# A two-layer hybrid encoder: second feed-forward product in seven block products, S5 tables a layer ahead, convolution in 32-wide tiles

## The chip, the cores and the metric

One NeuronCore of a Trainium2 chip runs the whole program. TensorE (PE) multiplies; its weight loads are listed apart as PEld. VectorE (DVE), ScalarE (ACT) and GpSimd (POOL) do elementwise work, SyncE (SP) issues all DMAs here. The metric is device time in microseconds (us), the median of several runs. A profile comes from one further execution.

## The reference

Two layers (`DEPTH = 2`), 1024 tokens, width 1024. A layer projects x to four head groups, joins them, and ends in a gated feed-forward part:

```python
h = jnp.einsum('bsd,de->bse', x, w_in[l])
y_a = conformer_conv(h[..., :OFF_S5], ...)      # GLU, depthwise conv of 31 taps, LayerNorm, silu
y_b = s5_mixer(h[..., OFF_S5:OFF_SC], ...)      # 16 groups, 64 complex states, both directions
y_c = short_gated_conv(h[..., OFF_SC:OFF_DA], sc_conv_w[l])
y_d = diff_attention(q, k, v, lam, da_subln_g[l], lam_init)   # 4 heads, two softmax maps each
mix = jnp.einsum('bse,ed->bsd', jnp.concatenate([y_a, y_b, y_c, y_d], axis=-1), w_out[l])
x = layer_norm(DEEPNORM_ALPHA * x + mix, ln1_g[l], ln1_b[l])
ff = jax.nn.silu(x @ w_ffn1[l]) * (x @ w_ffn3[l])
x = layer_norm(DEEPNORM_ALPHA * x + ff @ w_ffn2[l], ln2_g[l], ln2_b[l])
```

All is float32; the hidden width `FFN` is 2816, that is 22 blocks of 128.

## The kernel before

**Precision.** A large product is made of three: each operand is split into a rounded high part and the low rest (`split`, a cast and a subtraction), and `mm3` (L546) issues high by high, high by low and low by high, each a matmul of 128 rows, 128 columns of weights and up to 512 moving columns. Small products run in plain float32, where one matmul shows as two records.

**Order.** Every call goes through `Weaver`, which records it and then orders all instructions of the program by its own estimates, with a shift of priority for each step and layer (`SHIFT`) and a preference for the engine of an operation that several can do (`PREF`; `any2` is VectorE or GpSimd, `any3` also ScalarE). The result is a fixed list for each engine, worked off in that order. All instructions carry the line of `emit` (L471), so they are told apart by tile names.

**Stages of a layer.** `mixers_in` (L1519) runs through nine blocks of `w_in`: `tg` are token-major products, `cg` channel-major ones. Between them stand the S5 pairs: `s5_pair_tables` (L868) computes tables of a pair of groups (tile `s5t`), `s5_pair` (L926) uses them. The convolution (`conv_windows`, `conv_part`, `conv_norm`, L1068 to L1104) is a matmul for each of 256 channels (`cvo`): weights are a Toeplitz block of 128 rows and 96 columns, read by DMA with overlapping rows, and 11 windows of tokens move. Then come attention (`sc` scores, `atp` transposes, `po`) and the output product (`wo`), interleaved row block by row block.

**Feed-forward part.** `run` (L1581) goes over 11 chunks of 256 hidden columns. For w_ffn1 (q = 0) and w_ffn3 (q = 1), `ffn_up` (L1458) makes each 2 by 2 block product out of seven block products (`up`) instead of eight; `make_unit` (L1424) forms the seven weight operands of a group with four additions and splits each into one of four slots of `wring`. A group's raw weights (`upraw`) come in two buffers, which are reloaded once read. The second product (`dn`, `ffn_down` L1496) is direct: it is woven between the groups, chunk by chunk, each time adding to the rows in SBUF (`r`):

```python
for ci, (g, w2) in enumerate(chunks):
    for i in range(2):
        self.mm3(ps, g[:, 0, i, ts], g[:, 1, i, ts], w2[i][:, 0, :], w2[i][:, 1, :],
                 ci == 0 and i == 0, ci == len(chunks) - 1 and i == 1)
```

The last two chunks are added together, row block by row block, each followed by its LayerNorm.

Of the kernel before, what the change touches and what calls it, by code (L numbers as in the profile page):

```python
# [9 lines left out]
F32 = mybir.dt.float32  # L10
# [35 lines left out]
R_SW, R_LG, R_LB, R_GB, NROW = 0, 3, 4, 5, 6  # L46


CB, CWIN, NBLK, CG = 96, 128, 11, 9
NCK = -(-GW // CG)  # L50
WROW = CB + CWIN
CBANK = 43
# [16 lines left out]
class Weaver:  # L69
# [3 lines left out]
    SHIFT = {"None": -3232, "attn_finish0": 525, "attn_finish1": -8000, "attn_heads0": 2951, "attn_heads1": -4395,  # L73
# [12 lines left out]
    PREF = {"attn_finish0 gpsimd": -4310, "attn_finish0 scalar": -769, "attn_finish0 vector": 4528,  # L86
# [20 lines left out]
    CHUNK = 1370.0  # L107
    WINDOW = 3413.0
    SHARE = 0.42
    OUTS = ("out",)  # L110

# [373 lines left out]
class Trunk:  # L485
# [164 lines left out]
    def load_small(self, l):  # L650
# [3 lines left out]
        for r, k in ((R_LG, "conf_ln_g"), (R_LB, "conf_ln_b"), (R_GB, "s5_b_glu")):  # L654
            nc.sync.dma_start(raw[r:r + 1, :], t[k][l:l + 1, :])
# [735 lines left out]
    def weight_stream(self, l, order):  # L1391
# [3 lines left out]
        for item in order:  # L1395
# [4 lines left out]
            for u in range(n):  # L1400
                makers.append((g, u, u == n - 1))
# [318 lines left out]
```

## Time and profile before

| what | value |
|---|---|
| median of 3 runs | 2551.14 us (2549.97 to 2555.72) |
| the profiled execution, own time | 2548.31 us |
| its span, first to last instruction | 2546.5 us |
| TensorE busy | 2438.0 us, 96% |
| VectorE, GpSimd, ScalarE busy | 63%, 49%, 31% |
| mean granted TensorE clock | 0.964 of full |
| DMA | 193.53 MB, mean 76 GB/s |

A busy TensorE is not TensorE at its peak: its busy time is stretched where the granted clock is lower. A matmul's duration overlaps that of the next, so what one costs is read from the distance between starts, or from a group's busy time by its count.

### The profile page before, as it was taken

Reading aid. Unit: us, or ns where it says so; the run is one execution under the profiler, and the core shown is the slowest. Engines: PE = TensorE matmul, PEld = TensorE weight load, DVE = VectorE, ACT = ScalarE, POOL = GpSimd, SP = SyncE. Lnnn points to the kernel's source line nnn. Section 1 sums busy time; section 2 is a strip of 40 time slices with the busy share of each in tenths; the row PEclk is TensorE's granted clock in tenths of the full one; section 3 lists DMA queues with packets and bytes.
Section 4 is the critical chain, followed back from the end, with each engine's and each line's share of the span. In section 5 each row is a group of like instructions: output and inputs, shape, how many; then the busy total and the mean of one; then the engine's idle time right before and its main releaser. Section 6 shows DMA issues by size and latency. Waiting matters only on the chain. (4 is left out here: it accounts for less than half of the span.)

```text
span 2546.5 us, 34450 instructions
## 1 busy us (share of the span) xinstructions
PE 2438.0 (96%) x13464; PEld 2049.7 (80%) x13464; DVE 1592.5 (63%) x2559; ACT 795.2 (31%) x1343; POOL 1243.4 (49%) x1015
## 2 busy tenths in 40 slices
PE   8999989888999999999899999899989999999997
PEld 7889987677888888888688899777778888888885
DVE  6688348886555555555563785698855445554456
ACT  2200356543222222222231113555432222222231
POOL 2201373535566666565640004745376655555574
PEclk9998899999999999999899989999999999999998
DMA  6334321114111111111333342211241111111212
GB/s 165 100 90 132 98 73 51 60 51 155 53 53 55 50 50 58 51 53 55 113 114 85 85 124 91 73 63 55 72 132 58 53 56 52 56 50 50 58 53 96
DMA packets 193081, 193.53 MB, mean 76 GB/s; under 512 B 84878, under 2 KB 168088, under 8 KB 192664
## 3 DMA queue, kind: packets, MB, share of 16 engines
q1 hardware_dynamic: 192920, 191.34, 24.9%
q8 instruction: 106, 1.74, 0.3%
q14 instruction: 55, 0.45, 0.1%
HBM read 164.61 MB, written 26.71 MB: 75 GB/s over the span
## 5 line engine op out<-in xcount | busy, mean ns | idle before, releaser
L471 PE MATMUL up<-xT,wring 128*128 128x512 f32 x2112 | 485.9, 389 | 0.0
L471 PEld LDWEIGHTS up<-xT,wring 128*128 128x128 f32 x2112 | 396.4, 188 | 82.3
L471 PE MATMUL dn<-wring,g 128*128 128x512 f32 x1920 | 450.4, 391 | 3.9 <-POOL wring L471 3.1
L471 POOL TENSOR_TENSOR wring<-upraw,wring 128x512 fp32r<-128x512 f32 x220 | 311.5, 1418 | 250.4 <-ACT wring L471 250.1
L471 PEld LDWEIGHTS dn<-wring,g 128*128 128x128 f32 x1920 | 359.8, 188 | 83.3 <-POOL wring L471 6.6
L471 PE MATMUL up<-xB,wring 128*128 128x512 f32 x1584 | 370.0, 389 | 0.2 <-DVE xT L471 0.2
L471 PEld LDWEIGHTS up<-xB,wring 128*128 128x128 f32 x1584 | 297.3, 188 | 62.1 <-DVE xT L471 0.4
L471 DVE TENSOR_TENSOR r<-r,dn 128x512 f32<-128x512 f32 x288 | 197.9, 687 | 214.0 <-PE dn L471 214.0
L471 ACT CAST wring<-upraw 128x512 fp32r<-128x512 f32 x220 | 136.6, 621 | 469.8 <-PE dn L471 162.5
L471 PE MATMUL cg<-xh,win 128*128 128x512 f32 x640 | 220.9, 414 | 3.1 <-POOL win L471 1.9
L471 PE MATMUL tg<-win,xh 128*128 128x256 f32 x1024 | 203.0, 296 | 1.0 <-POOL win L471 0.6
L471 PE MATMUL wo<-wout,yhl 128*128 128x512 f32 x768 | 195.8, 400 | 0.0
L471 PEld LDWEIGHTS tg<-win,xh 128*128 128x128 f32 x1024 | 170.5, 202 | 3.2 <-POOL win L471 0.9
L471 ACT ACTIVATE probs<-sc,asm 128x1024 f32<-128x1024 f32 x128 | 143.2, 1120 | 91.8 <-DVE asm L471 91.7
L471 DVE TENSOR_REDUCE asm<-sc 128x1 f32<-128x1024 f32 x128 | 155.3, 1217 | 24.7 <-PE sc L471 24.3
L471 PEld LDWEIGHTS wo<-wout,yhl 128*128 128x128 f32 x768 | 142.1, 190 | 28.8 <-POOL yhl L471 0.3
L471 POOL TENSOR_TENSOR wring<-w2raw,wring 128x512 fp32r<-128x512 f32 x80 | 103.7, 1301 | 105.0 <-ACT wring L471 105.0
L471 PE MATMUL tg<-win,xl 128*128 128x256 f32 x512 | 153.2, 300 | 0.0
L471 PEld LDWEIGHTS cg<-xh,win 128*128 128x128 f32 x640 | 126.0, 197 | 32.7 <-issue 2.9
L471 POOL CAST win<-wraw 128x1024 fp32r<-128x1024 f32 x21 | 27.8, 1326 | 212.6 <-PE cg L471 160.1
L471 PE MATMUL cg<-xl,win 128*128 128x512 f32 x320 | 129.5, 405 | 0.0
L471 POOL TENSOR_TENSOR wring<-tw,wring 128x512 fp32r<-128x512 f32 x88 | 122.7, 1394 | 7.8 <-ACT wring L471 7.8
(232 smaller groups left out, 3851.1 us busy)
## 6 DMA issues: line engine op xcount, KB each, us to landing
upraw<-in_w_ffn_dram SPq DMA_DIRECT2D x88, 512.0 KB, 3.8
w2raw<-in_w_ffn_dram SPq DMA_DIRECT2D x44, 512.0 KB, 3.5
wraw<-in_w_in_dram SPq DMA_DIRECT2D x36, 512.0 KB, 4.5
ctap<-taps_scr SPq DMA_DIRECT2D x38, 432.0 KB, 4.9
woraw<-in_w_out_dram SPq DMA_DIRECT2D x16, 512.0 KB, 3.7
r<-x_scr SPq DMA_DIRECT2D x16, 512.0 KB, 4.0
conv<-taps_scr SPq DMA_DIRECT2D x18, 432.0 KB, 4.8
x_scr<-xr SPq DMA_DIRECT2D x14, 512.0 KB, 3.0
```

What stands on the lines that cost most here:

```text
L471: getattr(e, method)(*args, **kwargs)
```

## The change

**Second product in two phases.** `ffn_up` now runs over all 11 chunks first. Its products (`gst`) and four sums or differences of them (`down_operands`) are stored to memory (`a_scr`). Then the down phase takes seven block products, one after the other, each over 11 chunks: a unit n is 4 row tiles by one chunk, 12 matmuls. `down_prep`, called three units ahead, loads the unit's left operand (`araw`), forms the weight difference where there is one, and splits both sides into `aring` and `wring`; `down_out` adds a finished block product to the rows it belongs to. Rows are normalised after the sixth and the seventh product, four row blocks each.

**S5 tables.** Those of the second layer are computed during the first layer's chunks 0 to 7 and stored; the second layer loads them.

**Convolution.** A channel is now a matmul of 64 rows and 32 columns with 32 windows moving; two row halves and four column groups of the array alternate. The transposes that make the windows (`cvw`) go from 44 to 136. The normalisation over channels sums with a small matmul. **Order of blocks:** attention's v, q, k instead of k, v, q. The tables `SHIFT` and `PREF` have other numbers throughout.

```diff
-CB, CWIN, NBLK, CG = 96, 128, 11, 9
...
+CB, CWIN, NBLK, WROW = 32, 64, 32, 96
...
-    SHIFT = {"None": -3232, "attn_finish0": 525, "attn_finish1": -8000, "attn_heads0": 2951, "attn_heads1": -4395,
...
+    SHIFT = {"None": -7481, "attn_finish0": 1069, "attn_finish1": -7446, "attn_heads0": 1472, "attn_heads1": -6174,
...
+    def s5_ahead(self, l, pr):
...
+        self.s5_pair_tables(pr, False)
+        self.s5_store(pr)
...
+    def s5_store(self, pr):
+        self.nc.sync.dma_start(self.t5d[pr], self.s5t[pr % 2]["all"])
+
+    @step
+    def s5_load(self, pr):
+        R = self.s5t[pr % 2]
+        self.nc.sync.dma_start(R["all"], self.t5d[pr])
+        self.nc.sync.dma_start(R["M0"], self.m0d[pr].rearrange("j p g n -> (j p) g n"))
...
-                nc.tensor.matmul(ps[0:CB, h, (c - c0) * NBLK:(c - c0 + 1) * NBLK], lhsT=tap[:, k * CB:k * CB + CB], rhs=self.zT[:, :, c], start=True, stop=True)
...
+        for w0 in range(-2, NBLK, 4):
+            ps = self.b((P, 4, P), "cvw")
+            for i in range(min(4, NBLK - w0)):
...
+    def conv_part(self, l, ct):
...
+        for kb in (0, 32):
+            for a in range(2):
+                src = self.wrd[2 * l + ct, 64 * a + kb:64 * a + kb + 1, :]
+                nc.sync.dma_start(self.tapt[64 * a:64 * a + 64], bass.AP(src.tensor, src.offset, [[1, CWIN], [WROW, 32], [1, CB]]))
+            for k in range(kb, kb + 32):
+                j = k % 4
+                for a in range(2):
+                    r = slice(64 * a, 64 * a + 64)
+                    nc.tensor.matmul(ps[32 * j:32 * j + 32, a, k // 4, :], lhsT=self.zT[r, 64 * ct + k, :], rhs=self.tapt[r, k - kb, :],
+                                     start=True, stop=True)
...
-                nc.any2.tensor_tensor(s, s, dst, op=ALU.mult)
-                hi, lo = (rg[:, f, h].rearrange("p (i t s) -> p t i s", t=2, s=P)[:, t] for f in range(2))
-                self.split(s.rearrange("p (i s) -> p i s", s=P), hi, lo)
+                hv = lambda x: x.rearrange("p (r n) -> p r n", r=2)
+                nc.any2.tensor_tensor(G[:, h, :, t], hv(s), hv(dst), op=ALU.mult)
...
-    def ffn_down(self, chunks, j, n, r, first):
...
+    def down_operands(self, c, G, ad):
...
+        op = lambda o, a, b, f: nc.any2.tensor_tensor(U[:, o], U[:, a], U[:, b], op=f)
+        nc.sync.dma_start(ad[c, 0], U[:, 0])
+        op(4, 1, 3, ALU.add)
+        op(6, 0, 1, ALU.subtract)
+        op(5, 4, 0, ALU.subtract)
+        op(7, 2, 5, ALU.subtract)
...
+    DOWN = (("B11", 0), ("B21", 2), ("T1", 4), ("T3", 6), ("T2", 5), ("T4", 3), ("B22", 7))
...
+        b, u = self.DOWN[m]
+        if n % 2 == 0:
+            self.araw = self.raw([P, 2, 512], "araw")
+        a = self.araw[:, n % 2]
+        nc.sync.dma_start(a, ad[c, u])
+        w = lambda k: self.w2u(k, c)
+        if b in ("T1", "T3", "T2", "T4"):
+            x, y = {"T1": ("B12", "B11"), "T3": ("B22", "B12"), "T2": ("B22", "T1"), "T4": ("T2", "B21")}[b]
+            nc.any2.tensor_tensor(w(y), w(x), w(y), op=ALU.subtract)
+        sa, sb = self.aring[:, n % 4], self.bring[:, n % 4]
+        self.split(a, sa[:, 0], sa[:, 1])
+        self.split(w(b), sb[:, 0], sb[:, 1])
...
+        sa, sb = self.aring[:, n % 4], self.bring[:, n % 4]
+        for i in range(4):
+            s = slice(i * P, i * P + P)
+            self.mm3(ps[i], sa[:, 0, s], sa[:, 1, s], sb[:, 0], sb[:, 1], c == 0, c == NHID // 2 - 1)
...
+            elif m == 4:
+                add(r(0, i, 1), p)
+                add(u[i], p)
+                axpy(r(1, i, 0), u[i])
+                nc.any2.tensor_tensor(r(1, i, 1), r(1, i, 1), u[i], op=ALU.add)
...
-        return [OFF_S5, 0, GW, OFF_SC + GW, OFF_SC + 2 * GW, OFF_SC, OFF_DA + GW, OFF_DA + 2 * GW, OFF_DA]
+        return [OFF_S5, 0, GW, OFF_SC + GW, OFF_SC + 2 * GW, OFF_SC, OFF_DA + 2 * GW, OFF_DA, OFF_DA + GW]
...
-        self.s5_pair_tables(0)
+        tables = self.s5_pair_tables if l == 0 else self.s5_load
...
-            if pr % 3 == 0:
-                self.conv_part(l, pr // 3)
+            if pr < 2:
+                self.conv_part(l, pr)
+            elif pr == 3:
+                self.conv_norm(l, yT)
...
-        self.conv_norm(l, yT)
         for jp in range(4):
-            self.attn_k(xT, w(6), jp)
+            self.attn_v(xT, w(6), jp)
...
-            order = [("up", 0, 0), ("up", 0, 1)]
-            for c in range(1, NC):
-                order += [("up", c, 0)] + ([("down", c - 1)] if c < NC - 1 else []) + [("up", c, 1)]
-            self.weight_stream(l, order + [("down", NC - 2)])
...
+            self.weight_stream(l, [(c, q) for c in range(NC) for q in range(2)])
...
+            if l + 1 < DEPTH:
+                self.s5_ahead_alloc(l + 1)
             for c in range(NC):
...
+                self.ffn_up(1, X, sg, G)
+                self.down_operands(c, G, ad)
+                if l + 1 < DEPTH and c < 8:
+                    self.s5_ahead(l + 1, c)
...
+                if n + 3 < 7 * NC:
+                    self.down_prep(n + 3, ad)
...
+                self.down_unit(n, ps)
...
+                    if m >= 5:
+                        for i in range(4):
+                            j = 4 * (m == 5) + tile_of[i]
+                            self.layer_norm(rj(j), g2, b2, out[j] if l + 1 == DEPTH else x2d[j], 1 + (m == 6))
```

How the order moves. TensorE, the first layer's feed-forward part, chunks 0 and 1; first before (`up` and `dn` as above), then with the change (`s5wp` and `s5k` belong to the tables of the second layer):

```order
L471 MATMUL up_650<-xT_480_561,wring_597 128x512 x12
L471 MATMUL up_651<-xT_482_563,wring_597 128x512 x12
L471 MATMUL dn_655<-wring_597,g_598 128x512 x6
L471 MATMUL dn_656<-wring_597,g_598 128x512 x6
L471 MATMUL dn_657<-wring_597,g_598 128x512 x6
```

```order
L473 MATMUL up_656<-xB_492_577,wring_612 128x512 x6
L473 MATMUL s5wp_657<-ident,s5a_636 128x128 x4
L473 MATMUL up_656<-xB_492_577,wring_612 128x512 x6
L473 MATMUL s5k_658<-s5a_635,s5a_636 48x144 x4
L473 MATMUL up_661<-xB_487_572,wring_612 128x512 x12
```

Groups of `up` now follow each other without `dn` between them, with eight small matmuls for the tables once a chunk.

SyncE's queue in the same place; before (`w2raw` are raw weights of the second product), then with the change:

```order
L471 DMA upraw_636<-in_w_ffn_dram 128x4x256
L471 DMA upraw_637<-in_w_ffn_dram 128x4x256
L471 DMA w2raw_647<-in_w_ffn_dram 128x1024
L471 DMA w2raw_648<-in_w_ffn_dram 128x1024
L471 DMA upraw_653<-in_w_ffn_dram 128x4x256
```

```order
L473 DMA s5t_scr<-s5a_635 128x1600
L473 DMA m_scr<-s5a_636 16x8x128
L473 DMA upraw_664<-in_w_ffn_dram 128x4x256
L473 DMA m_scr<-s5a_636 16x8x128
L473 DMA a_scr<-gst_634 128x512
L473 DMA upraw_665<-in_w_ffn_dram 128x4x256
L473 DMA a_scr<-gst_634 128x6x512
L473 DMA upraw_673<-in_w_ffn_dram 128x4x256
```

The loads of raw weights now stand behind stores of tables and of products.

TensorE where attention of the first layer begins; before, then with the change (`ktp` and `qtp` transpose k and q):

```order
L471 MATMUL tg_272<-win_88,xl_7_87 128x256
L471 MATMUL tg_272<-win_88,xh_5_85 128x256 x2
L471 MATMUL sc_297<-kst_154_235,stg_234 128x512 x2
L471 MATMUL sc_298<-kst_154_235,stg_234 128x512 x2
L471 MATMUL tg_272<-win_88,xl_7_87 128x256
```

```order
L473 MATMUL tg_285<-win_92,xl_7_91 128x256
L473 MATMUL ktp_281<-ident,stg_264 128x128 x4
...
L473 MATMUL ktp_290<-ident,stg_264 128x128 x4
L473 MATMUL qtp_308<-ident,stg_264 128x128 x4
L473 MATMUL qtp_309<-ident,stg_264 128x128 x4
L473 MATMUL sc_312<-kst_180_265,stg_264 128x512 x2
```

Before, 85 matmuls of `tg` stand behind the first `sc`, between the scores of the first row block; with the change all `tg` stand ahead of it.

## Rows read from the trace of the kernel before

**Rows 1.** The profile's first part: busy time, share of the span, instructions.
```profile
span 2546.5 us, 34450 instructions
PE 2438.0 (96%) x13464; PEld 2049.7 (80%) x13464; DVE 1592.5 (63%) x2559; ACT 795.2 (31%) x1343; POOL 1243.4 (49%) x1015
```
**Rows 2.** Windows: length, busy time (instructions) per engine, granted clock, DMA share, GB/s.
```profile
core 0: us, PE busy (x) PEld busy (x) DVE busy (x) ACT busy (x) POOL busy (x), PEclk, DMA share, GB/s
110.00:300.00 190.00, 189.31 (x1319) 171.17 (x1318) 133.46 (x303) 26.78 (x54) 34.23 (x42) 0.87 0.39 104
260.00:270.00 10.00, 10.00 (x57) 10.00 (x57) 3.75 (x10) 0.00 (x0) 0.00 (x0) 0.50 0.77 201
350.00:400.00 50.00, 39.08 (x297) 32.66 (x296) 41.06 (x46) 31.43 (x57) 33.82 (x34) 0.93 0.22 72
1360.00:1540.00 180.00, 179.90 (x1242) 160.70 (x1241) 127.63 (x300) 28.60 (x52) 2.96 (x8) 0.88 0.39 105
1866.80:2480.00 613.20, 613.20 (x2707) 507.71 (x2706) 306.51 (x384) 180.19 (x301) 378.95 (x276) 1.00 0.18 55
```
**Rows 3.** The chain of waits, in the second feed-forward part: start, length, what.
```profile
1866.84 54.46 PE up L471 x240
1921.30 10.88 PE dn L471 x48
```
**Rows 4.** Groups by form on PE: tiles, shapes, count | busy us, mean ns.
```profile
L471 PE MATMUL dn<-wring,g 128*128 128x512 f32 x1920 | 450.4, 391 | 3.9 <-POOL wring L471 3.1 <-DVE r L471 0.8
L471 PE MATMUL dn<-w2b,g 128*128 128x512 f32 x192 | 55.6, 425 | 8.8 <-DVE w2b L471 5.5 <-POOL w2b L471 3.2
L471 PE MATMUL cvo<-convz,ctap 128*96 128x11 f32 x700 | 72.7, 245 | 0.0
L471 PE MATMUL cvo<-convz,conv 128*96 128x11 f32 x324 | 35.2, 248 | 0.0
L471 PE MATMUL po<-aT,vq 128*64 128x128 f32 x1024 | 64.9, 280 | 0.0
L471 PE MATMUL cvw<-ident,conv 128*128 128x128 f32 x44 | 6.2, 273 | 0.1
```
**Rows 5.** Timeline of PE: start, length, instruction; three places.
```profile
36.95 1.13 PE L471 MATMUL s5cps<-ident,s5b 16*128 16x16 f32 x16
...
347.22 0.40 PE L471 MATMUL tg<-win,xh 128*128 128x256 f32 x2
347.46 0.28 PE L471 MATMUL tg<-win,xl 128*128 128x256 f32 x1
347.58 0.40 PE L471 MATMUL tg<-win,xh 128*128 128x256 f32 x2
```
**Rows 6.** Windows of the convolution's matmuls alone (tile cvo): PE, PEld, DVE busy, clock.
```profile
170.00:190.00 20.00, 6.98 (x80) 7.11 (x80) 0.00 (x0) 1.00 0.46 122
```
**Rows 7.** Timeline of POOL, second layer's feed-forward part.
```profile
1897.37 1.29 POOL L471 TENSOR_TENSOR wring<-upraw,wring 128x512 fp32r<-128x512 f32 x1 [0.80 <-ACT wring L471]
1900.56 1.29 POOL L471 TENSOR_TENSOR tw<-upraw,upraw 128x512 f32<-128x512 f32 x1 [1.90 <-DMA upraw<-in_w_ffn_dram]
...
1908.64 1.74 POOL L471 TENSOR_TENSOR wring<-upraw,wring 128x512 fp32r<-128x512 f32 x1
```
**Rows 8.** Groups by form on DVE.
```profile
L471 DVE TENSOR_TENSOR xc<-x1row 128x512 f32<-128x512 f32 x4 | 2.7, 674 | 0.0
L471 DVE TENSOR_TENSOR sg<-sg,tw 128x512 f32<-128x512 f32 x66 | 101.5, 1537 | 1.6
L471 DVE TENSOR_TENSOR tu<-tu,up 128x512 f32<-128x512 f32 x110 | 75.0, 682 | 24.7 <-PE up L471 23.6
L471 DVE TENSOR_TENSOR s5t<-P 128x256 f32<-128x256 f32 x94 | 42.0, 461 | 1.4
```
**Rows 9.** Timeline, ends of the two feed-forward parts.
```profile
1231.70 1.20 PE L471 MATMUL dn<-wring,g 128*128 128x512 f32 x4
...
1249.54 1.54 PE L471 MATMUL dn<-w2b,g 128*128 128x512 f32 x6
```
**Rows 10.** Timeline, the last matmuls and the last rows' normalisation.
```profile
2532.15 1.52 PE L471 MATMUL dn<-w2b,g 128*128 128x512 f32 x6
...
2541.50 1.41 DVE L471 SCALAR_TENSOR_TENSOR r<-r,rs,ln 128x512 f32<-128x512 f32 x2 [0.46 <-POOL rs L471]
```

More of the change, by code (lines that the diff above doesn't have):

```diff
@@ L264, in cost @@
                 return max(85.0, 0.4167 * n + 13.3), 0
-            pair = int(outs[0].shape[0]) == 64
-            return max(128.0, 0.4167 * 4 * n + 5) * (0.57 if pair else 1.0), 0
+            k, m = int(kw["lhsT"].shape[0]), int(outs[0].shape[0])
+            if k == 64 and m == 32:
+                return 40.0, 0
+            return max(128.0, 0.4167 * 4 * n + 5) * (0.57 if m == 64 else 1.0), 0
         if eng == "sync":
@@ L867, in s5_pair_tables @@
     @step
-    def s5_pair_tables(self, pr):
+    def s5_pair_tables(self, pr, here=True):
         nc = self.nc
@@ L1017, in conv_alloc @@
         T = self.convt = self.S([P, SROW], F32, "conv")
[L1019 removed]
+        self.zp = [T[:, c * 1040:c * 1040 + 1040] for c in range(2)]
         for z in self.zp:
             self.nc.gpsimd.memset(z[:, 0:16], 0.0)
[L1022 removed]
     def z_half(self, ct, hf):
@@ new lines, in conv_part @@
+    @step
+    def conv_part(self, l, ct):
+        nc = self.nc
+        ps = self.d((P, 2, 16, CB), "cvo")
+        for kb in (0, 32):
[8 more added lines that the diff above has]
+                                     start=True, stop=True)
+        y = self.zTt[:, 1024 * ct:1024 * ct + 1024].rearrange("p (a s t) -> p a s t", a=2, t=CB)
+        cb = self.cb[:, 32 * ct:32 * ct + 32].rearrange("p (a s) -> p a s", a=2)
+        for a in range(2):
+            nc.vector.tensor_tensor(y[:, a], ps[:, a], cb[:, a].unsqueeze(2).to_broadcast([P, 16, CB]), op=ALU.add)
@@ L1133, in conv_norm @@
-        for ct in range(2):
-            nc.sync.dma_start(yT[ct].rearrange("p (j c) -> p j c", j=NJ), out[ct])
+        nc = self.nc
+        v = nc.vector
+        yT_ = lambda t: t.rearrange("p (s t) -> p t s", t=CB)
+        y, q, o = self.zTt[:, 0:2048], self.zTt[:, 2048:SROW], self.zTt[:, 2048:SROW]
+        st = self.cst
+        gsum = lambda ps, x: nc.tensor.matmul(ps, lhsT=self.grp4.rearrange("p j w -> p (j w)"), rhs=x, start=True, stop=True)
+        bc = lambda x: x.unsqueeze(1).to_broadcast([P, 64, CB])
@@ new lines, in conv_norm @@
+        nc.gpsimd.tensor_tensor(st[:, 3], st[:, 3], self.cexp, op=ALU.pow)
+        xn = q.rearrange("p (t s) -> p t s", t=CB)
+        v.tensor_tensor(xn.rearrange("p t s -> p s t"), yv, bc(st[:, 3]), op=ALU.mult)
+        o = y.rearrange("p (j e c) -> p j e c", j=4, e=4)
+        for th in range(4):
+            ps = self.b((P, 4, 4, CB), "cvb")
+            for e in range(4):
+                t0 = 8 * th + 2 * e
+                self.tr(ps[:, e].rearrange("p j w -> p (j w)"), xn[:, t0:t0 + 2, :].rearrange("p t s -> p (t s)"))
+            for j in range(4):
+                nc.scalar.activation(o[:, j, :, 3 - th::4], ps[:, :, j, :], AF.Silu, scale=self.cprm[:, 0, j:j + 1], bias=self.cprm[:, 1, j:j + 1])
@@ L1137, in short_c @@
+        for h in range(2):
+            dst = yT[0:2].rearrange("q p (a n) -> (q p) a n", a=NJ)[:, 7 - h::-2, :]
+            nc.sync.dma_start(dst.rearrange("(s j) e n -> s j e n", j=4), o[64 * h:64 * h + 64])
     @step
@@ L1398, in weight_stream @@
                 prev["next"] = g
-            n = 7 if item[0] == "up" else 4
-            for u in range(n):
-                makers.append((g, u, u == n - 1))
+            for u in range(7):
+                makers.append((g, u, u == 6))
             prev = g
@@ L1549, in mixers_in @@
         self.s5_ring()
-        self.s5_pair_tables(0)
+        tables = self.s5_pair_tables if l == 0 else self.s5_load
+        tables(0)
         nxt(2)
@@ L1558, in mixers_in @@
         gi = 0
-        self.conv_windows(l)
+        for ct in range(2):
+            self.conv_windows(l, ct)
         for pr in range(8):
-            if pr % 3 == 0:
-                self.conv_part(l, pr // 3)
+            if pr < 2:
+                self.conv_part(l, pr)
+            elif pr == 3:
+                self.conv_norm(l, yT)
             self.s5_pair(pr)
             if pr + 2 < 8:
-                self.s5_pair_tables(pr + 2)
+                tables(pr + 2)
             e = len(gem) * (pr + 1) // 8
@@ L1624, in run @@
             self.wring = self.S([P, 4, 2, 512], F32R, "wring")
-            rg = self.S([P, 2, 2, SEQ], F32R, "g")
-            r = [self.S([P, 4, D], F32, "r") for _ in range(2)]
             rows = []
@@ L1657, in run @@
-            g2, b2 = self.gain_rows(t["ln2_g"], t["ln2_b"], l, "ln2")
-            wring, self.wring = self.wring, self.S([P, 4, 2, 512], F32R, "w2b")
-            self.weight_stream(l, [("down", NC - 1)])
-            w2b = self.take(4)
-            if l + 1 < DEPTH:
-                xT = self.new_xT()
-                self.in_ring(l + 1)
-            for j in range(NJ):
-                for n in range(2):
-                    self.ffn_down([(rgs[0], w2a[2 * n:2 * n + 2]), (rgs[1], w2b[2 * n:2 * n + 2])], j, n, rj(j), False)
-                self.layer_norm(rj(j), g2, b2, out[j] if l + 1 == DEPTH else x2d[j], 1 + (j == NJ - 1))
-                if l + 1 < DEPTH:
-                    self.to_xT(j, rj(j), xT)
+                self.ffn_up(1, X, sg, G)
@@ new lines, in run @@
+                self.down_operands(c, G, ad)
+                if l + 1 < DEPTH and c < 8:
+                    self.s5_ahead(l + 1, c)
+                if c == NC - 2:
+                    self.w2_tiles((1, 2))
+                    self.load_w2(l, "B11", range(NC))
+                    self.load_w2(l, "B21", range(2))
+            self.w2_tiles((3, 0, 4, 5))
+            r = [self.S([P, 4, D], F32, "r") for _ in range(2)]
+            self.aring, self.bring = self.S([P, 4, 2, 512], F32R, "aring"), self.wring
```

319 lines of the change are left out of this document (182 added, 137 removed), and 68 rows, old and new, of tables (PREF, SHIFT).

## The prediction

> **What bounds the kernel now.** I read the page's first part, then stretches of the span, then the chain of waits, then groups and timelines where the change works. TensorE is busy for 2438.0 of 2546.5 us [rows 1], so the time is what TensorE has to do plus some 108 us in which it waits. In nearly all of the second feed-forward part it never pauses (613.20 busy in 613.20 us) and the granted clock is full [rows 2]; there a taken-out matmul is worth its whole distance between starts. The chain gives that distance: 240 `up` in 54.46 us and 48 `dn` in 10.88 us, 0.227 us each [rows 3]. In the two stretches with S5 and convolution TensorE is busy too, but at a granted clock of 0.87 and 0.88, and ten microseconds of nothing but convolution run at 0.50, the lower of its two levels [rows 2]. So there a busy TensorE is not one at its peak. Where attention starts it is busy for 39.08 of 50 us, VectorE for 41.06 [rows 2]. And at the end of a feed-forward part 24 `dn`, 5.4 us of work, are spread over 17.8 us [rows 9].
>
> The sum is made against the profiled execution, 2548.31 us; the median of the runs is 2.8 us above it.
>
> **Term 1, second product.** Seven block products for eight: 2 layers x 7 x 11 units x 12 = 1848 `dn` instead of 2112. 264 x 0.227 [rows 3] = **-59.8**. These matmuls have the old shape, so the bounds are narrow; what can eat the gain is the feeding (terms 5 to 7).
>
> **Term 2, convolution.** The old one takes 72.7 + 35.2 = 107.9 us [rows 4] for 512 matmuls of two records. The new one has 512 matmuls of 64 rows, 32 columns and 32 moving columns, a shape that no row shows. The nearest rows from both sides: `po`, 64.9 us for 512 matmuls that move 128 columns [rows 4], 127 ns each, scaled to 32 columns 32 ns; and `s5cps`, 16 tiny records one behind the other in 1.13 us [rows 5], (1.13 - 0.21) / 15 = 61 ns a record, 122 ns a matmul. The old ones alone at full clock take 6.98 us for 80 records [rows 6], 87 ns a record with 11 moving columns. I take 85 ns a matmul, between the two ends, nearer the second since small records plainly have a floor here: 512 x 0.085 = 43.5. The windows need 92 more `cvw` at 6.2 / 44 = 0.141 us [rows 4], +13. Together **-51** (bounds -78 and -32).
>
> Here the rows show a floor near 61 ns a record. The Trainium skill, TensorE: Matmul & The Clock Gate, section Wait — 56ns, not 53.3ns?, puts the least distance of two starts at about 25 ns however few columns move; by it two records would be 50 ns and the convolution 25.6 us, 18 us below my term, an estimate from that page. The rows of `s5cps` do not bear that out, and the sum goes without it.
>
> **Term 3, clock.** 190 us at 0.87 and 180 us at 0.88 [rows 2] are 0.13 x 190 + 0.12 x 180 = 46 us lost to the clock. The convolution's own part, 107.9 - 1024 x 0.087 = 18.5 [rows 4, 6], is already in term 2. Of the other 28 us I take **-12** (0 to -28): S5's small work stays there, but its tables in the second layer go, and with them pauses.
>
> **Term 4, start of attention.** The 85 `tg` that now stand between the first scores cost three per 0.36 us [rows 5], 10.2 us a layer, and filled time in which TensorE waited for VectorE. Standing ahead, they no longer fill it; the new order (v, q, k) needs its last block in transposed form at once. Of 20.4 us I take **+14** (0 to +20), since VectorE, 41.06 of 50 busy [rows 2], is also relieved a little of other work.
>
> **Term 5, up phase of the first layer.** The 14 subtractions for low parts and 8 additions of a chunk's weights are all GpSimd's there. Alone such an operation takes 1.29 us, beside VectorE 1.74 [rows 7]. VectorE gets the S5 tables, some 18 operations of 0.461 us a chunk [rows 8], 8 operations on `gst` and 14 sums out of PSUM at 0.682 [rows 8]. GpSimd: 22 x 1.29 + 26 x 0.45 = 40.1 us. VectorE, stretched as `sg` is from 674 to 1537 ns [rows 8]: 14 x 0.682 + 8 x 1.54 + 18 x 1.05 = 40.8. TensorE needs 2 x 84 x 0.227 = 38.1 us a chunk. So both engines are just over: 2.7 x 8 chunks = **+22** (0, where overlap costs less, to +50). The few matmuls of the tables are as many as before and cost nothing anew.
>
> **Term 6, feed of the down phase.** A unit is 2.72 us. In the second layer VectorE has the 154 subtractions, 44 differences, 66 casts and 28 sums: 264 x 0.674 + 28 x 0.682 = 197 us of 77 x 2.72 = 209.5 [rows 3, 8], with GpSimd's casts beside it. I take **+12** over both layers (0 to +60). The new loads and stores, about 40 MB a layer, raise a DMA share of 0.18 [rows 2] to at most 0.4 and hide behind preparation three units (8.2 us) ahead. If a store stands before a raw load in SyncE's queue that cover goes (rival D).
>
> **Term 7, first units of a down phase** wait for their splits, which stand behind the last chunk's: **+8** (0 to 25, twice what rows 9 show at such a handover).
>
> **Term 8, the old ends.** The `dn` of the last chunks vanish with their stalls: 8.8 us of waits, and 192 x (55.6/192 - 450.4/1920) = 10.6 of stretch [rows 4, 9]: **-19**.
>
> **Term 9, the new ends.** Four rows are normalised behind the last matmul instead of one. After the last `dn` one row takes from 2533.67 to 2546.5; VectorE's last operation of it 1.41 us [rows 10]. Three more rows in a pipeline are between 3 x 1.41 = 4 and 3 x 12.8 = 38; I take +8, and +6 between the layers, where other work is there: **+14**.
>
> Sum: -59.8 - 51 - 12 + 14 + 22 + 12 + 8 - 19 + 14 = -71.8, so 2476.5 for a profiled execution and **2479 us** for the median.
>
> **The rivals.** **A, feeding hides altogether:** terms 5 and 6 are nothing and the convolution reaches 32 ns: 2479 - 34 - 27 = 2418. For it: GpSimd waits for loads and ScalarE in the old part [rows 7], so it has slack. Against: VectorE's `sg` at 1537 ns [rows 8].
>
> **D, SyncE's queue:** raw loads stand behind stores that wait for VectorE. A GpSimd wait of 1.90 us for a raw load is there already [rows 7]; 2 us more at each of 16 groups is +32, 2511. The old queue has no stores between these loads, so no row speaks against it.
>
> **C, the convolution does not get cheaper:** many small matmuls at the old 107.9 us (+64) and no clock regained (+12): 2555, no change. For it: the floor of `s5cps` [rows 5]. Against: that floor gives 62 us, not 108.
>
> **B, slower: VectorE and GpSimd take turns at SBUF.** In the first layer's up phase a chunk is then 28.4 + 18 x 0.461 + 8 x 0.674 = 42.1 us, with a wait of 1.90 at each of two groups [rows 7] 45.9, 7.8 over TensorE's 38.1; 8 chunks are 62 instead of 22. In the second layer's down phase 197 us of VectorE and GpSimd's casts and differences, some 60 us by its 1.29 [rows 7], stand one behind the other: 257 for 209.5, +48 instead of the 8 I have for it. Together 2479 + 80 = 2559. It decides once these two phases lose 77 us beyond my terms. Against it: a subtraction beside VectorE takes 1.74 us, less than 1.29 + 0.67 = 1.96 [rows 7, 8]. The Trainium skill, SBUF — State Buffer, section SBUF: two separate sides, says that the two engines' shared ports are an exclusive lock held for a whole instruction, which is this rival; the 1.74 in the trace is near it but does not reach it.
>
> **How the numbers follow.** The forecast has 0.60, A 0.13, D 0.12, C 0.06, B 0.09. Forecast, A and D are faster. A measurement tells 0.2%, 5 us, from no change: 2546 to 2556. Faster 0.85, same 0.06 (C), slower 0.09 (B). The range leaves out B and C (0.15) and a little of A's lower end: below, the convolution's and the feeds' lower bounds reach past A, to 2410; above, D with the upper half of term 5 or 6 gives 2535.
>
> **What would show it.** Right: the convolution's group near 44 us at 512 matmuls and a granted clock over 0.9 around it; `dn` at 0.227 us in steady units; pauses of 2 to 3 us a chunk on TensorE in the first layer's chunks 0 to 7, none in 8 to 10; a tail of some 20 us behind the last matmul. Wrong: TensorE without pauses in that up phase (A), its waits ending with a raw load behind stores (D), a clock still at 0.5 and a group of `cvo` over 90 us (C), GpSimd's subtractions above 1.9 us and TensorE pausing in most units of the second layer's down phase (B).

## The result and the profile after

The changed kernel takes 2512.22 us (median of 4 runs, 2509.15 to 2518.04), the kernel before 2550.55 in the same comparison: ratio 0.9854, 95% interval 0.9825 to 0.9883. That is 38 us faster; 72 were forecast. The profiled execution has a span of 2510.3 us. The first part of its page [rows 1]:

```profile
span 2510.3 us, 34996 instructions
PE 2306.7 (92%) x13300; PEld 1905.1 (76%) x13300; DVE 1936.2 (77%) x2989; ACT 704.6 (28%) x1227; POOL 1096.4 (44%) x957
```

TensorE has 131 us less to do, but it waits 204 us instead of 108. So TensorE lost more work than forecast, and most of that gain was given back as waits. The windows by stage, with the columns of [rows 2], tell where. Each layer has the stretch ahead of the first score, then attention with the output product, then the feed-forward part; at the end comes the tail behind the last matmul. The kernel before:

```profile
0.00:348.20 348.20, 335.73 (x2302) 301.46 (x2303) 213.53 (x610) 79.17 (x141) 91.64 (x103) 0.92 0.41 111
348.20:612.20 264.00, 226.58 (x1568) 184.49 (x1566) 223.91 (x295) 142.21 (x253) 126.19 (x107) 0.95 0.23 79
612.20:1292.10 679.90, 670.60 (x2946) 550.40 (x2947) 389.48 (x486) 173.99 (x280) 426.96 (x315) 0.99 0.20 62
1292.10:1606.40 314.30, 312.90 (x2185) 281.62 (x2185) 189.35 (x429) 71.72 (x116) 54.00 (x71) 0.93 0.35 99
1606.40:1866.50 260.10, 229.25 (x1568) 185.46 (x1566) 226.40 (x297) 135.79 (x244) 133.76 (x115) 0.95 0.24 82
1866.50:2533.70 667.20, 662.97 (x2906) 546.26 (x2904) 343.40 (x435) 191.06 (x312) 406.14 (x305) 0.99 0.19 57
2533.70:2546.50 12.80, 0.00 (x0) 0.00 (x0) 6.45 (x10) 1.24 (x1) 4.75 (x5) 0.58 0.31 123
```

The changed kernel, where the feed-forward part has two rows, up phase and down phase:

```profile
0.00:327.90 327.90, 295.35 (x2436) 256.75 (x2436) 243.76 (x599) 100.16 (x185) 103.18 (x114) 0.97 0.35 94
327.90:597.90 270.00, 219.17 (x1480) 174.85 (x1480) 233.36 (x329) 139.39 (x245) 106.73 (x90) 0.91 0.18 58
597.90:1050.70 452.80, 438.80 (x1946) 356.02 (x1944) 299.92 (x411) 135.07 (x232) 338.54 (x237) 1.00 0.38 124
1050.70:1284.90 234.20, 220.11 (x948) 177.47 (x948) 185.72 (x219) 77.29 (x129) 138.92 (x108) 0.98 0.45 150
1284.90:1571.10 286.20, 270.18 (x2237) 235.93 (x2236) 153.99 (x249) 82.15 (x140) 61.64 (x92) 0.97 0.33 100
1571.10:1828.10 257.00, 222.81 (x1480) 178.59 (x1481) 227.14 (x317) 124.47 (x223) 101.80 (x83) 0.91 0.18 60
1828.10:2250.00 421.90, 420.62 (x1854) 347.11 (x1852) 356.88 (x527) 42.00 (x70) 128.68 (x115) 1.00 0.36 116
2250.00:2489.90 239.90, 219.62 (x925) 178.40 (x924) 219.09 (x317) 4.03 (x7) 109.83 (x115) 0.95 0.39 135
2489.90:2510.30 20.40, 0.01 (x1) 0.00 (x0) 16.36 (x28) 0.00 (x0) 7.04 (x9) 0.60 0.33 129
```

| stage | before | after | difference |
|---|---|---|---|
| first layer, up to the first `up` | 612.2 | 597.9 | -14.3 |
| first layer, feed-forward | 679.9 | 687.0 | +7.1 |
| second layer, up to the first `up` | 574.4 | 543.2 | -31.2 |
| second layer, feed-forward | 667.2 | 661.8 | -5.4 |
| tail | 12.8 | 20.4 | +7.6 |

The two feed-forward parts together gain nothing, though 264 matmuls are gone. Three groups on TensorE, by form, answer to [rows 4]:

```profile
L473 PE MATMUL dn<-wring,aring 128*128 128x512 f32 x1848 | 437.2, 398 | 31.9 <-DVE aring L473 10.4 <-DVE wring L473 9.4 <-POOL wring L473 4.2
L473 PE MATMUL s5y<-s5t,s5k 128*128 128x128 f32 x128 | 20.7, 279 | 4.5 <-DVE s5k L473 4.5
L473 PE MATMUL cvo<-ctap,convz 64*32 64x32 f32 x1024 | 11.5, 200 | 0.9 <-DMA ctap<-taps_scr 0.8
```

The convolution fell from 107.9 us to 11.5. And `dn` now waits 31.9 us. By the starts of the units on TensorE's timeline, counted from 0 within each block product, 12 matmuls take 2.72 us, just as forecast, in at least 61 of the first layer's 77 units and 67 of the second's. Most of what is lost lies in a few places: the first unit of the phase (5.6 and 4.4 us in the two layers), units 7 and 8 of the first block product (4.8 and 9.2 us in the first layer, 4.8 and 11.4 in the second), the start of the fourth (first unit 4.5 and 8.2) and the last (in the second layer unit 4 with 11.6). In the first layer's up phase chunks 0 to 7, which carry the tables, take about 42 us (40.8 to 45.4), chunks 8 to 10 38.1 to 38.2.

### The profile page after: what moved, and what is told of

Its sections match the earlier page's. It is cut to its first block, busy times and chain, and to the rows that moved or that the text cites. A ratio compares the mean times of both kernels' runs of the same rounds, so it can differ in the third digit from the quotient of the medians.

```text
span 2510.3 us, 34996 instructions
## 1 busy us (share of the span) xinstructions
PE 2306.7 (92%) x13300; PEld 1905.1 (76%) x13300; DVE 1936.2 (77%) x2989; ACT 704.6 (28%) x1227; POOL 1096.4 (44%) x957
## 5 line engine op out<-in xcount | busy, mean ns | idle before, releaser
L473 PE MATMUL dn<-wring,aring 128*128 128x512 f32 x1848 | 437.2, 398 | 31.9 <-DVE aring L473 10.4
L473 PEld LDWEIGHTS dn<-wring,aring 128*128 128x128 f32 x1848 | 353.4, 192 | 114.5 <-DVE aring L473 11.9
L473 PE MATMUL cg<-xh,win 128*128 128x512 f32 x640 | 211.9, 401 | 3.7 <-DVE p L473 2.9
L473 PE MATMUL tg<-win,xh 128*128 128x256 f32 x1024 | 194.7, 289 | 3.2 <-DVE sca L473 1.4
L473 POOL TENSOR_TENSOR wring<-upraw,wring 128x512 fp32r<-128x512 f32 x110 | 166.5, 1519 | 55.4 <-ACT wring L473 54.2
L473 DVE TENSOR_TENSOR aring<-araw,aring 128x512 fp32r<-128x512 f32 x141 | 135.7, 968 | 43.4 <-ACT aring L473 36.9
L473 PEld LDWEIGHTS tg<-win,xh 128*128 128x128 f32 x1024 | 162.6, 194 | 6.6 <-DVE sca L473 1.8
L473 DVE TENSOR_REDUCE asm<-sc 128x1 f32<-128x1024 f32 x128 | 155.2, 1216 | 14.7 <-PE sc L473 13.0
L473 ACT ACTIVATE sg<-sg 128x512 f32<-128x512 f32 x88 | 55.2, 632 | 255.5 <-DVE sg L473 255.5
L473 DVE TENSOR_TENSOR wring<-w,wring 128x512 fp32r<-128x512 f32 x135 | 116.4, 863 | 9.5 <-ACT wring L473 6.8
L473 PE MATMUL sc<-kst,stg 128*128 128x512 f32 x256 | 95.3, 466 | 28.9 <-ACT probs L473 27.9
```

The source lines that it names most:

```text
L473: getattr(e, method)(*args, **kwargs)
```

## Experiments: why the feed-forward part gains nothing

There are two theories for the down phase. By Q, data come late because of the order of SyncE's queue. By V, VectorE is short of time.

**Late loads.** SyncE's timeline at the start of the second layer's down phase, changed kernel:

```profile
2255.70 0.32 SPq L473 DMA_DIRECT2D araw<-a_scr  x1
2256.98 13.34 SPq L473 DMA_DIRECT2D w<-in_w_ffn_dram  x15
2270.64 0.92 SPq L473 DMA_DIRECT2D araw<-a_scr  x2
...
2273.18 1.08 SPq L473 DMA_DIRECT2D a_scr<-gst  x2
2274.87 10.33 SPq L473 DMA_DIRECT2D araw<-a_scr  x3
```

Fifteen weight loads stand ahead of the left operands of the next units, and TensorE then waits for what is made of these operands:

```profile
2276.86 0.73 PE L473 MATMUL dn<-wring,aring 128*128 128x512 f32 x2 [1.96 <-POOL aring L473]
2283.84 8.33 PE L473 MATMUL dn<-wring,aring 128*128 128x512 f32 x24 [6.24 <-DVE aring L473]
```

In the longer of the two waits VectorE was not idle. It worked off six weight differences, which use the early loads, ahead of the left operand's subtraction:

```profile
2279.49 3.69 DVE L473 TENSOR_TENSOR w<-w,w 128x512 f32<-128x512 f32 x6
2283.10 1.28 DVE L473 TENSOR_TENSOR aring<-araw,aring 128x512 fp32r<-128x512 f32 x2
```

The edit ties those loads, in the order only, to the unit before (`unit` is its last matmul):

```diff
-                        self.load_w2(l, b, (n - n0,))
+                        self.load_w2(l, b, (n - n0,), unit)
...
                         nc.sync.dma_start(rj(j), x1d[j])
+                        nc.ops[-1].deps.add(unit)
```

> The changed kernel, but the loads of second-product weights and of rows in the down phase are issued no earlier than the unit at which the code asks for them, so that the stores and loads of the left operand are not behind them. Theory Q (order of SyncE's queue and the burst of loads at the start of a down phase): units 7 and 8 of the first block product, now 4.8 and 9.2 us in the first layer and 4.8 and 11.4 in the second, fall to 2.72; 17 us less, 2495 us. Theory V (VectorE is short of time): those units stay, 2512 us.

Measured: 2506.09 us, 6 less than the changed kernel where 17 less were expected. The interval of its ratio to the kernel before, 0.9779 to 0.9853, overlaps the changed kernel's, so the time alone doesn't show a gain. The units do: units 7 and 8 are at 2.72 in both layers, as Q says. Whether late data or the six differences in VectorE's list cost more there, the run does not separate, since the edit takes both away. In the second layer the fourth block product now starts with units of 16.6 and 5.0 us. TensorE's waits in that phase:

```profile
PE dn L473 <- DVE wring L473: 16.7, 8, 6.3
PE dn L473 <- DVE r L473: 4.7, 1, 4.7
```

The weight differences, which need those loads, now come later too, and TensorE waits for VectorE there instead. So V holds in the same phase.

**ScalarE's casts.** In the second layer's down phase ScalarE is busy for 4.03 of 239.9 us, VectorE for 219.09, most of it with the subtractions for low parts:

```profile
L473 DVE TENSOR_TENSOR wring<-w,wring 128x512 fp32r<-128x512 f32 x75 | 63.2, 844 | 2.0 <-POOL wring L473 1.9
L473 DVE TENSOR_TENSOR aring<-araw,aring 128x512 fp32r<-128x512 f32 x73 | 61.8, 850 | 2.7 <-POOL aring L473 0.5
```

The edit gives ScalarE all the casts of that phase: 64 that VectorE had (34.7 us) and 81 that GpSimd had (69 us). The first layer is as it was.

```diff
-        self.split(a, sa[:, 0], sa[:, 1])
-        self.split(w(b), sb[:, 0], sb[:, 1])
+        for x, y in ((a, sa), (w(b), sb)):
+            (nc.scalar if self.layer == 1 else nc.any3).copy(y[:, 0], x)
+            nc.any2.tensor_tensor(y[:, 1], x, y[:, 0].bitcast(F32), op=ALU.subtract)
```

> The changed kernel, but all rounding casts of the second layer's down phase are ScalarE's, which is idle there (4 of 240 us busy). Theory V (VectorE is short of time there): the pauses at the start of the fourth block product (5.5 us) and in unit 4 of the last (8.9 us) go, and 12 to 15 us with them, 2498 us; units 7 and 8 of the first stay. Theory Q: they come from late data, and the time stays at 2512 us.

Measured: 2494.82 us, 17 less, as V says. The fourth block product has no pause any more, the last has 1.2 us instead of 9.3; units 7 and 8 stay (6.6 and 7.8). The phase, in the columns of the windows above:

```profile
2247.60:2469.20 221.60, 213.21 (x924) 174.38 (x923) 170.11 (x246) 86.00 (x151) 48.22 (x33) 0.98 0.41 142
```

VectorE's mean subtraction falls only from 844 to 741 ns (`wring`) and from 850 to 799 (`aring`). Whether the casts taken off VectorE or those taken off GpSimd matter more is not separated.

**Both.** The two edits together.

> The changed kernel with late loads and ScalarE's casts together. If the two losses are separate (late data in units 7 and 8 of the first block product, VectorE short of time in the fourth and the seventh), the second layer's down phase comes to 212 us and the first layer's to 228: 2512 - 17 - 14 = 2481 us. If late loads only move VectorE's differences into a later place, where they are in the way again, it stays near 2490.

Measured: 2484.03 us, ratio to the kernel before 0.9731 (0.9702 to 0.9761): the fastest version here. The down phases take 227.5 and 219.6 us; in the second layer 9.0 us are left at the fourth block product. So both causes are real, and their gains, 6 and 17 alone and 28 together, add up within the noise.

**A further step that fails.** Also the second layer's differences on GpSimd, and two of the last four rows normalised the other way:

```diff
-            nc.any2.tensor_tensor(w(y), w(x), w(y), op=ALU.subtract)
+            (nc.gpsimd if l == 1 else nc.any2).tensor_tensor(w(y), w(x), w(y), op=ALU.subtract)
...
-                            self.layer_norm(rj(j), g2, b2, out[j] if l + 1 == DEPTH else x2d[j], 1 + (m == 6))
+                            self.layer_norm(rj(j), g2, b2, out[j] if l + 1 == DEPTH else x2d[j], 1 + (m == 6 and i > 1))
```

> The changed kernel with late loads, ScalarE's casts, the second layer's weight differences on GpSimd, and two of the last four rows normalised on ScalarE and GpSimd as well. If the remaining 9 us at the start of the fourth block product of the second layer are VectorE's, they go, and the tail of 20 us gets shorter by 3 to 6: 2484 - 12 = 2472 us. If GpSimd's differences slow VectorE's subtractions as much as they free it, 2484 us.

Measured: 2500.78 us, 17 more than with the two edits above, where a gain was expected. VectorE's subtractions in that phase, first with the two edits above, then with GpSimd's differences:

```profile
L473 DVE TENSOR_TENSOR aring<-araw,aring 128x512 fp32r<-128x512 f32 x73 | 58.7, 804 | 40.7 <-ACT aring L473 40.7
L473 DVE TENSOR_TENSOR wring<-w,wring 128x512 fp32r<-128x512 f32 x74 | 58.2, 786 | 0.0
```

```profile
L473 DVE TENSOR_TENSOR aring<-araw,aring 128x512 fp32r<-128x512 f32 x73 | 79.9, 1094 | 36.1 <-ACT aring L473 36.1
L473 DVE TENSOR_TENSOR wring<-w,wring 128x512 fp32r<-128x512 f32 x74 | 70.0, 946 | 0.0
```

Their means go from 804 to 1094 and from 786 to 946 ns. That is 33 us more, against 25.8 us of differences taken away from VectorE. Between the two profiled executions, 20 us apart, the phase is 4 us longer and the tail another 4; the other 12 lie in stretches that the edit doesn't touch and are not explained. The two parts of the edit were not run apart.

**The tables in their own layer.** Second layer's tables computed in its own mixers:

```diff
-        tables = self.s5_pair_tables if l == 0 else self.s5_load
+        tables = self.s5_pair_tables
...
-                if l + 1 < DEPTH and c < 8:
-                    self.s5_ahead(l + 1, c)
```

> The changed kernel, but the second layer computes its S5 tables in its own mixers, as before. In the changed kernel chunks 0 to 7 of the first layer's up phase take 42.1 us each and chunks 8 to 10 38.1. Theory 1: the tables cost more there than they save in the second layer; then all eleven chunks take 38.1 (33 us less) and the second layer's stretch ahead of the scores grows by about 20: 2500 us. Theory 2: the move pays, because the second layer's stretch is bound by VectorE when it has the tables too: it grows by 45 and the sum is 2525 us.

Measured: 2513.94 us, no difference, and between the two theories. The first layer's up phase and the second layer's stretch ahead of the scores:

```profile
593.80:1014.80 421.00, 420.11 (x1851) 347.34 (x1849) 228.27 (x266) 124.87 (x206) 333.43 (x238) 1.00 0.36 117
1246.60:1571.90 325.30, 289.93 (x2334) 251.56 (x2333) 205.98 (x411) 91.48 (x164) 72.59 (x99) 0.94 0.26 73
```

The up phase is 32 us shorter, the other stretch 39 us longer. GpSimd is as busy as with the tables (333 us), and TensorE hardly ever pauses, so the 22 GpSimd operations a chunk fit. What the tables cost in the up phase is 18.7 us more of busy TensorE, with 95 more records, and 13 us of waits, mostly for VectorE's table operations.

The tables have one more price, and it lies ahead of the up phase. In the changed kernel TensorE's longest pause stands right before the first layer's first `up`:

```profile
593.21 3.30 PE L473 MATMUL xop<-ident,xc 128*128 128x128 f32 x12 [18.51 <-DVE xc L473]
```

VectorE's list has the first table operations (`s5a`) ahead of the last rows' normalisation (`xr`, `xc`), on which these transposes wait:

```profile
575.58 6.94 DVE L473 TENSOR_TENSOR s5a<-s5a 128x288 f32<-128x288 f32 x9 [1.47 <-DMA s5a<-p_scr]
...
585.63 3.17 DVE L473 TENSOR_TENSOR s5a<-s5a 128x256 f32<-128x256 f32 x9
588.73 0.74 DVE L473 SCALAR_TENSOR_TENSOR xr<-xr,mv,ln 128x512 f32<-128x512 f32 x1
```

With the tables in their own layer the longest such wait is 4.7 us, and the first layer's attention stretch takes 260.1 us instead of 270.0. So early tables cost 32 + 10 us in the first layer, about the 39 that they save in the second. Tables a layer ahead that start behind that normalisation were not run.

## Experiments: what the convolution is worth

**The old convolution in the changed kernel.**

```diff
-CB, CWIN, NBLK, WROW = 32, 64, 32, 96
+CB, CWIN, NBLK, CG = 96, 128, 11, 9
...
-            if pr < 2:
-                self.conv_part(l, pr)
+            if pr % 3 == 0:
+                self.conv_part(l, pr // 3)
```

> The changed kernel with the convolution of before (256 channels of 128 rows, 96 columns, 11 windows). Theory 1: the new convolution is worth what TensorE's busy time fell by, 107.9 to 11.5 us less 14 for more window transposes, so this kernel takes 2512 + 82 = 2594 us. Theory 2: more than half of that gain came back as waits in the same stretches (TensorE's idle time ahead of the first scores rose from 14 to 49 us over both layers), so it takes about 2512 + 30 = 2542 us, with those stretches again without pauses.

Measured: 2614.27 us, 102 more; the theory nearest to it had 82, so its mechanism is there, and 20 us beyond it. Both stretches ahead of the scores are longer by TensorE's busy time (350.1 and 324.3 us, at a granted clock of 0.91 and 0.90, for 295.4 and 270.2 at 0.97).

**The new convolution alone** in the kernel before.

```diff
-CB, CWIN, NBLK, CG = 96, 128, 11, 9
+CB, CWIN, NBLK, WROW = 32, 64, 32, 96
...
-            if pr % 3 == 0:
-                self.conv_part(l, pr // 3)
+            if pr < 2:
+                self.conv_part(l, pr)
+            elif pr == 3:
+                self.conv_norm(l, yT)
```

> The kernel before with the new convolution and nothing else of the change. Theory 1 (from the run with the old convolution, 102 us slower than the changed kernel): the convolution alone is worth about 100 us, so 2551 - 100 = 2451 us, faster than the whole change, whose other parts then lose about 60 us. Theory 2: those 102 us were the old convolution's bad fit to the changed order, and alone it is worth the fall of TensorE's busy time less new waits, 40 to 60 us: 2491 to 2511 us.

Measured: 2566.98 us, ratio 1.0056 (1.0036 to 1.0076): slower than before. Both theories fall. The two stretches:

```profile
0.00:344.90 344.90, 303.36 (x2352) 259.32 (x2353) 231.49 (x588) 98.04 (x182) 103.98 (x101) 0.92 0.30 80
...
1296.00:1628.10 332.10, 285.01 (x2237) 243.98 (x2236) 192.01 (x394) 92.30 (x161) 63.70 (x75) 0.91 0.23 63
```

TensorE is busy 60 us less but waits 41.5 and 47.1 us instead of 12.5 and 1.4. Its longest waits in the two stretches:

```profile
PE s5y L470 <- DVE s5k L470: 16.0, 10, 4.6
...
PE s5y L470 <- DVE s5k L470: 11.0, 6, 4.8
PE cvb L470 <- DVE convz L470: 9.6, 1, 9.6
```

`s5y` uses what VectorE's chain of an S5 pair leaves in `s5k`; it waited 0.3 us for it before and 4.5 in the changed kernel. The long convolution had stood beside that chain and covered it. Of the 89 us of waits some 41 belong to S5, some 15 to the new convolution's own normalisation in the second layer (`cvb` and what follows it); the rest is spread. The granted clock of the two stretches, 0.92 and 0.91, is not above the 0.92 and 0.93 of the kernel before, so the rest gets no faster.

**The old order of blocks** in the changed kernel, with its old priorities:

```diff
-        return [OFF_S5, 0, GW, OFF_SC + GW, OFF_SC + 2 * GW, OFF_SC, OFF_DA + 2 * GW, OFF_DA, OFF_DA + GW]
+        return [OFF_S5, 0, GW, OFF_SC + GW, OFF_SC + 2 * GW, OFF_SC, OFF_DA + GW, OFF_DA + 2 * GW, OFF_DA]
```

> The changed kernel with attention's blocks in the old order (k, v, q) and their old priorities, so that products of the last block stand behind the first scores again. Theory 1: the new order costs what TensorE's idle time rose by in the two stretches of attention (37 to 51 and 31 to 34 us) and ahead of them in the waits for the copies of the last block (some 12 us), so 2512 - 25 = 2487 us. Theory 2: the waits move, and the products that fill the first row block would have been done anyway: 2507 to 2517 us.

Measured: 2543.11 us, 31 more, against both theories. `s5y` waits 16.0 us in the first layer, as in the kernel with the convolution alone:

```profile
PE s5y L473 <- DVE s5k L473: 16.0, 10, 4.6
```

The windows of the first layer from the first `s5v` to the last `s5y`, the stretch of the S5 pairs, show what stands in the chain's gaps: the changed kernel, then this run, then the convolution alone.

```profile
125.00:288.80 163.80, 154.92 (x1434) 138.28 (x1434) 141.28 (x282) 31.88 (x64) 42.71 (x45) 0.99 0.25 64
128.70:294.90 166.20, 140.13 (x1255) 121.13 (x1254) 143.88 (x280) 28.93 (x59) 46.94 (x41) 0.93 0.24 63
129.00:295.10 166.10, 141.00 (x1255) 121.70 (x1254) 144.00 (x280) 28.95 (x59) 46.64 (x41) 0.92 0.24 63
```

The stretch takes nearly the same time in all three, with VectorE busy for 141 to 144 us of it. TensorE does 179 more matmuls in it in the changed kernel, all of them `tg` (467 instead of 288), and is idle for 8.9 us instead of 26. So products of an attention block, moved ahead of the scores, fill the gaps of VectorE's chain. That is their order and their priorities together; the two were not separated.

**All but the second product and the tables**: the kernel before with the new convolution, the new order of blocks and the new numbers of `SHIFT` and `PREF` for all steps ahead of the feed-forward part.

> All but the second product and the tables: the kernel before with the new convolution, the new order of blocks and the new priorities ahead of the feed-forward part. Theory 1: convolution and order are worth something only together, since products of a block without transposes fill the waits that the S5 chain leaves once the long convolution is gone; the stretches up to the first `up` take 598 and 586 us instead of 612 and 574, and the sum is near 2551 (2540 to 2555). Theory 2: they give the second layer also what it got in the changed kernel, 543 us for that stretch, without its tables being moved: 2551 - 14 - 31 = 2506 us.

Measured: 2534.56 us, 0.9935 (0.9911 to 0.9958), 18 less than before: 14.7 less in the first layer up to the first `up`, 1.2 in the second. The first layer comes out as the first theory says (597.5 us, 598 expected); the second, 573.2, lies between the theories (586 and 543), as the time does.

**Only the second product**: the changed kernel with the old convolution, the tables in their own layer, and the old order and priorities ahead of the feed-forward part.

> Only the second product in two phases: the changed kernel with the old convolution, the tables in their own layer, the old order of blocks, and the old priorities ahead of the feed-forward part. Theory 1: the two phases give what the stages show, some 26 us less in the first layer's feed-forward part without tables (680 to 654), 5 less in the second's, 8 more behind the last matmul: 2551 - 23 = 2528 us. Theory 2 (the terms of the sum for this part alone: -59.8 for the products, -19 for the old ends, +20 for the feeding, +14 for the new ends): 2506 us.

Measured: 2580.07 us, 1.0105 (1.0075 to 1.0135): slower by 28, and both theories fall. The feed-forward parts take 667.2 and 669.5 us (before 679.9 and 667.2), and the tail is 8 longer. The second layer's stretch up to the first `up` is 26 longer: in its first part TensorE waits 10 us more and is busy 15 us longer, at a granted clock of 0.89 instead of 0.93. The single parts do not add up. -18 and +28 would be +10, but the run with all of the change except the tables' move is 40 us faster than the kernel before in its own comparison. What brings the other 50 us is left open.

One rival is untested for all the mixed kernels of this section. The numbers in `SHIFT` and `PREF` belong to each whole kernel, and these runs use numbers of one kernel with steps of the other. So part of what they lose can be a bad fit of the numbers; nor was there a run with the new numbers alone.

**One column group at a time.** Conv matmuls sorted, 8 in a row in the same part of the array:

```diff
-            for k in range(kb, kb + 32):
-                j = k % 4
-                for a in range(2):
+            for a in range(2):
+                for k in sorted(range(kb, kb + 32), key=lambda k: k % 4):
+                    j = k % 4
```

> The changed kernel with the convolution's 512 matmuls in another order: 8 one behind the other in the same row half and column group, instead of alternating over the eight. If matmuls in different parts of the array overlap, and that is why a record takes 11 ns, they now stand behind one another, some 40 to 61 ns a record as in the small matmuls of the S5 setup, 1024 records in 40 to 60 us, and the time is 30 to 50 us longer. If a record of this size simply takes 11 ns, the group stays at 11.5 us and the time at 2512.

Measured: 2538.11 us, 26 more; the group takes 29.0 us. Both are less than expected, in the expected direction. Sixty records in the changed kernel, then here:

```profile
118.85 0.72 PE L473 MATMUL cvo<-ctap,convz 64*32 64x32 f32 x60
```

```profile
117.73 1.78 PE L473 MATMUL cvo<-ctap,convz 64*32 64x32 f32 x60
```

With 0.193 us for the last one, records start every (0.72 - 0.19) / 59 = 9 ns alternating and every 27 ns in one place. The group explains 17.5 of the 26 us; the rest is not explained.

## Why the forecast was half right

The kernel got faster, by about half of what was forecast, and the time lay in the range. That it lay there is in part luck. The sum was 33 us too good, but single terms were off by as much as that, in both directions, and the largest loss ahead of the feed-forward part was no term at all. By stages, a ledger of what was measured closes. In the feed-forward parts terms 1 and 8 gave -59.8 and -30.5. The down phases took 55 us more than their matmuls' own distance (terms 6 and 7), the first layer's up phase 33.9 more (term 5) and the second's 3.0, so the parts come to +1.7. Ahead of them TensorE was busy for 97 us less and waited 51.5 us more, which is -45.5. The tail was +7.6.

- **Term 1 (-59.8)** was right: units of 2.72 us, the old distance between matmuls.
- **Term 2 (-51)** was mis-sized: `cvo` went from 107.9 to 11.5 us and `cvw` from 6.2 to 24.1, together -78, at the lower bound. The step that failed was the choice of 85 ns a matmul by nearness to `s5cps`. One behind the other in one place, the new matmuls take 29.0 us, 57 ns each and 27 ns a record, so the 61 ns a record of `s5cps` were no floor for this shape; why those are so slow is not shown. Overlap in other parts of the array brings the group to 22.5 ns a matmul. The window of ten microseconds at a clock of 0.50 was also misread as nothing but convolution: it holds 35 `cvo` and 20 `tg`.
- **Term 3 (-12)**: the granted clock in the stretches ahead of the scores rose from 0.92 and 0.93 to 0.97. In their windows `cg` went from 245.2 to 233.7 us and `tg` from 213.9 to 204.5: 21 regained, not 12. But it fell elsewhere, in attention from 0.95 to 0.91 and in the down phases to 0.98 and 0.95, so the mean over the whole kernel stayed, 0.964 before and 0.963 after.
- **Missing term.** TensorE's waits ahead of the scores rose from 14 to 49 us, +35. I costed the convolution as if nothing stood beside it. The run with it alone shows the cover: 89 us of waits where there were 14, 41 of them for S5. In the changed kernel the products of attention fill most of that; of its +35 us, 14 are for the transposes of k and q, 7 for S5, 5 for the new convolution, and the rest is scattered.
- **Term 4 (+14)** missed the larger effect, and with it the sign of the whole. The waits in attention did rise (68 to 85 us), but some 14 of these 17 are for `xop` in the first layer, which is the tables' doing; waits of the scores rose by 13 and those of `atp` fell by 12.5. The cost that the term names, the last block's transposes, came ahead of the scores as the 14 us above. Against that, the same products fill gaps of the S5 chain: undoing the order, with its priorities, costs 31 us.
- **Term 5 (+22)**: in the up phase there were pauses only in chunks 0 to 7, as forecast, but 13 us, and mostly for VectorE; GpSimd's 22 operations a chunk fit. The tables' matmuls (18.7 us) moved, as I had counted. The 10 us at the end of attention, where table operations stand ahead of the normalisation, are in no term.
- **Terms 6 and 7 (+20)** came to 234.2 + 239.9 - 419.0 = 55 us. One step that failed was "hide behind preparation three units (8.2 us) ahead". It holds in at least 128 of 154 units, but not at the start of the phase, where weight loads stand ahead of the left operands. The other was VectorE's 197 us: it was busy for 219.09, since its 148 subtractions took 844 to 850 ns on average and not 674, and no time was left where a block product's end came on top. I had looked for rival D's mechanism in the up phase; the queue's order mattered in the down phase.
- **Term 8 (-19)** was -30: the old feed-forward parts are 679.9 and 667.2 us for 2904 matmuls each, which need 2904 x 0.2267 = 658.3. That is 21.6 and 8.9 us beyond the matmuls' own distance, with pauses and small transposes in it; the term had counted the `dn` alone.
- **Term 9 (+14)**: the tail grew by 7.6 (8 forecast). The +6 between the layers can't be told from terms 6 and 7.

Rival B, VectorE and GpSimd taking turns, did not come: GpSimd's subtractions took 1.61 us on average, under 1.9, and TensorE paused in about 10 of the 77 units of the second layer's down phase. VectorE's subtractions do get longer where GpSimd has more to do, from 804 to 1094 and 786 to 946 ns in the run with GpSimd's differences; but where VectorE was short of time it was enough to give ScalarE the casts. Rival D's 2511 us is nearest to the measured 2512, by coincidence: in the up phase GpSimd still waits about 2.0 us for raw loads at each of 13 groups, as the 1.90 before, but TensorE's waits there end with VectorE and ScalarE. Of rival A the first half came (the convolution fell below its 32 ns), not the second; of rival C nothing did.

## What to carry to other kernels

Before crediting TensorE with a shorter piece of work, name what ran beside it on the other engines. The gain ends where their chain becomes visible, and other work moved next to that chain may decide whether the shortening is worth anything. When a second phase begins, read the DMA queue in order: loads that are needed ten units later can stand ahead of those that are needed next. When work is moved to an earlier stage, look at what now stands behind it in an engine's list at the border of the two stages. If an engine is idle in the very phase where another is short, move a simple step to it first, before any restructuring.

## What the runs showed that I had not expected

Small matmuls of 64 rows and 32 columns in alternating parts of the array start every 9 ns, and every 27 ns in one part. The Trainium skill, TensorE: Matmul & The Clock Gate, section Wait — 56ns, not 53.3ns?, gives a floor of about 25 ns between starts; the 27 ns of the run in one part agree with it, the 9 ns of the alternating one go below it. The Trainium skill, TensorEngine Tiling (Array Packing), section Key Properties, says that different tiles can load weights and multiply in parallel; the 9 against 27 ns agree with that.

The same stretch of an unchanged order varied between profiled executions, from 327.9 to 334.5 us ahead of the first layer's scores, wider than some effects looked for here; differences under some 7 us are not read from single profiles.
